# Own buffers and another pace for a depthwise convolution's products, and a layer norm that is queued when its last tile is whole

## The chip, the cores and the metric

The kernel runs on one core of a Trainium2 chip. Its time is the device time of one execution in microseconds; the forecast is made on the median of such runs. The core has TensorE (PE in the profile) for matrix products, VectorE (DVE), ScalarE (ACT) and GpSimd (POOL) for elementwise work, and SyncE (SP), whose queue issues nearly all loads here. Each engine runs its own instructions in order; semaphores tie them together. TensorE writes to PSUM, which this kernel cuts into eight buffers of 128 x 512 f32.

## The reference

One sequence of 512 tokens, 1024 channels, f32, goes through two blocks. The first block has a mixer (the part that the change touches), then 32 routed experts (the best two of one group for each token). The second block has an mLSTM mixer, a short convolution mixer and two squared-ReLU MLPs. The first mixer:

```python
h = rms_norm(x, norm_mix_g)
proj = h @ w_in + b_in                                   # 1024 -> 6144 columns
a, z, gate_logits = split(proj, [2048, 4096])
# conformer branch
a1, a2 = split(a, 2);  a = a1 * sigmoid(a2)
y = causal_depthwise_conv(a, conv_w, width=31) + conv_b  # 31 taps, each channel by itself
y_a = silu(layer_norm(y, ln_g, ln_b)) @ w_conv_out + b_conv_out
# spatial gating branch
u, v = split(gelu(z), 2);  v = layer_norm(v)
sv = einsum("hqk,bnkhc->bnqhc", w_s * mask, v) + b_s     # inside blocks of 128 tokens
y_b = (u * sv) @ w_sg_out + b_sg_out
g_a, g_b = split(sigmoid(gate_logits), 2)
x = x + (g_a * y_a + g_b * y_b) @ w_out + b_out
```

The layer norm of the conformer branch runs over all 1024 channels, so it needs every channel tile of the convolution.

## The kernel before, in words

Activations lie with 128 channels on the partitions and 512 tokens along the free axis, so a matrix of 1024 channels is eight tiles. A dense product makes one tile of 128 outputs by 512 tokens from eight tiles of input. Weights and inputs are held as pairs of f16 numbers, high and low, so each step is three products (`wh` with the high and with the low input, `wl` with the high one), and a tile is 24 products of 128 x 512. The weights arrive as f32 chunks by SP's queue; ScalarE makes the high part `wh` (L275) and VectorE the low part `wl` (L279), a chunk every two tiles.

The first mixer's dense products follow each other on TensorE in this order: `wa` (16 tiles, the convolution's input and its gate in turn), `wv` (8, tokens on partitions), `wu` (8), `wgb` and `wga` (8 each, the two gates), `wsgo`, `wco` and `wo` (8 each). ScalarE or VectorE empties each finished PSUM buffer: `ut` at L731 for `wu`, `gate` at L761 for both gates.

The order of all other work is made by a planner in the program itself. It keeps a clock `clk` that advances with the products as they are written down (512 columns count as 512/2400 us). `at(delay, fn)` hangs a piece of work into the order `delay` later on that clock. Two lists of fillers are worked off while dense products are written: one filler each time that the clock has passed a due time, which then moves on by `pace`. One list holds the even channel tiles of the convolution, the other the odd ones:

- even tiles: the sum stands in a PSUM buffer. One filler begins it on ScalarE, 30 fillers add one tap each on VectorE (L640, `yc<-ap,cw,yc`), and the last one copies it to SBUF on ScalarE (L647) and calls `conv_done`.
- odd tiles: one filler begins the sum on ScalarE (L627). Each of the 30 others is two instructions: ScalarE multiplies the shifted input by the tap's weight into a buffer `tap` (L622), and GpSimd adds that buffer to the sum (L623).

`conv_done` adds the finished tile to `ya` on GpSimd (L609, L611). The layer norm takes `ya` from there: `ln_mu` sums it over the partitions on TensorE (`cs`), `ln_sub` spreads the mean with four transposes (`bc`), subtracts it and adds up the squares, `ln_r` makes the reciprocal root, and `ln_out` multiplies, applies SiLU and makes the f16 pairs `ch` that the product `wco` reads.

`tap` buffers come from the pool `t2`, whose 48 buffers of 2 KB per partition serve nearly all working tiles of the mixer. Whoever takes a buffer of `t2` next waits until its last reader is done.

The spatial mixing is hung into `wgb`: for each of eight heads, four f32 products (`mix`) on TensorE, and on VectorE a scale and add out of PSUM (L744, `s`), a product with `ut` (L748), and the low part of an f16 pair (L750, `sh`), whose high part ScalarE makes (L749).

In the kernel before, fillers come every 1.5 (even) and 1.4 (odd) on the planner's clock. After `wgb` the program flushes the hung work, works off what is left of the fillers, and then hangs the layer norm at fixed places into `wga` (22, 25 and 40 after its begin) and `ln_out` 4 into `wsgo`.

Of the kernel before, what the change touches and what calls it, by code (L numbers as in the profile page):

```python
# [17 lines left out]
P = 128  # L18
T = 512
# [18 lines left out]
# ---------------------------------------------------------------- host layout  # L38
# [77 lines left out]
# ---------------------------------------------------------------- device  # L116
# [4 lines left out]
class Net:  # L121
    def __init__(self, ctx, tc, x, cols, rows, wd, we, wr, wsg, out):
        self.tc, self.nc = tc, tc.nc
        self.din = dict(x=x, cols=cols, rows=rows, wd=wd, we=we, wr=wr, wsg=wsg)
        self.out = out
        pool = lambda n, b, **k: ctx.enter_context(tc.tile_pool(name=n, bufs=b, **k))
        self.cp = pool("const", 1)
        self.t2p = pool("t2", 48)
        self.sp = pool("small", 2)
        self.wp = pool("w32", self.W32)  # L130
        self.hp = pool("whl", self.WHL)
        self.pp = pool("ps", 8, space=bass.MemoryType.PSUM)
        ctx.enter_context(tc.manual_schedule())
        self.uid = 0
        self.fillers = [], []
        self.due, self.pace = [0.0, 0.0], (1.0, 1.0)
        self.items = []
        for c in range(NDENSE):
            if c == N1:
                self.items += [("e", j) for j in range(NPAIR * 12)]  # L140
            self.items.append(("d", c))
        self.w32, self.whl, self.late = {}, {}, {}
        self.stop = len(self.items)
        self.nload = self.nsplit = self.cur = 0
        self.clk = 0.0
        self.last_split = -100.0
        self.queue = []
        self.open = False
        self.live = set()
# [7 lines left out]
    # ---- allocation  # L157
# [17 lines left out]
    # ---- the order of issue: TensorE's queue is the clock, the rest is hung into it  # L175
# [30 lines left out]
    # ---- weight stream  # L206
# [5 lines left out]
    def place(self, c):  # L212
        """where expert chunk c goes (the weight buffers, those of the split weights, or, at first, working tiles),
        and the chunk that was there before"""
        w, h, t = self.W32, self.WHL - 2, self.EXTRA
        rnd, rest = w + h + t + 2, w + h + 2
        if c < self.ROUNDS * rnd:
            r, before = c % rnd, c - rnd
        else:
            r = (c - self.ROUNDS * rnd) % rest  # L220
            before = c - rest
            if r >= w + h:
                r += t
            elif c < self.ROUNDS * rnd + rest:
                before -= t
        return "w" if r < w else "t" if w + h <= r < w + h + t else "h", before
# [16 lines left out]
    def more(self):  # L243
        """the working tiles are free to take expert chunks"""
        self.open = True
        self.loads()
# [67 lines left out]
    # ---- building blocks  # L314
# [5 lines left out]
    def dense(self, base, plan, rhs, evac, tail=None):  # L320
        """out tile m [P features, tokens] = W[:, m].T @ x over eight k tiles; two m tiles in a chunk.
        plan: (mode, tiles): "m" a tile at a time, "k" a group with k outside, "hk" as "k" for the first
        half of the tokens and as "m" for the second, "hh" the first half of all tiles, then the second"""
# [77 lines left out]
    def dense_tok(self, base, rhs, evac):  # L401
        """out [P tokens, 512 columns] for four token tiles, two column halves"""
# [19 lines left out]
    def colsum(self, tile_, s=FULL, dst=None):  # L422
        """[P tokens, tiles] in PSUM: the sum over partitions of a tile [P, tokens]"""
# [7 lines left out]
    def rsqrt(self, src, scale, eps, n, s="rs", pool=False):  # L431
        """1 / sqrt(src * scale + eps), a tile [P, n]"""
# [13 lines left out]
    def bcast(self, cols):  # L446
        """[P, n, P] in PSUM: each column as a row, on every partition"""
# [21 lines left out]
    # ---- constants  # L469
# [35 lines left out]
    # ---- first mixer  # L505
    def first_mixer(self):
# [6 lines left out]
        # the first chunks run on x * g, not yet divided by the norm  # L513
# [53 lines left out]
        # gated convolution branch: a pair of tiles, then the depthwise convolution as filler work,  # L567
        # the even tiles on VectorE with the sum in PSUM, the odd ones on ScalarE and GpSimd
# [3 lines left out]
        # layer norm over channels (partitions) of the convolution output  # L572
        ch = []

        def ln_mu():
            mu = self.sm([P, NT], s="mu")
            nc.vector.tensor_scalar(mu, self.colsum(ya), 1.0 / D, None, op0=OP.mult)
            st["mu"] = mu

        def ln_sub():  # L580
# [7 lines left out]
            st["a"] = a  # L588

        def ln_r():  # L590
            st["r"] = self.rsqrt(self.colsum(st["a"]), 1.0 / D, EPS, NT, pool=True)

# [13 lines left out]
        def conv_done(m):  # L606
# [3 lines left out]
            elif len(whole) > 2:  # L610
                nc.gpsimd.tensor_add(ya, ya, yc[m])  # L611

        def conv(m, ap):
            b = v("conv_b")[:, m:m + 1]
            yc[m] = self.t2([P, T], s="yc")
            if m % 2:
                y = yc[m]

                def tap(j):
                    q = self.t2([P, T], s="tap")  # L620
# [47 lines left out]
        # rows for the spatial gating  # L668
# [28 lines left out]
        self.pace = self.PACE[0]  # L697
        self.dense(CBASE["wa"], [("m", range(4, 16))], hn, ev_a)

        # spatial gating: v with tokens on partitions  # L700
# [10 lines left out]
        self.pace = self.PACE[1]  # L711
# [21 lines left out]
        self.pace = self.PACE[2]  # L733
        self.dense(CBASE["wu"], [("m", range(KD))], hn, ev_u)

        # spatial mixing inside blocks of 128 tokens, a head is a tile of channels
# [18 lines left out]
        # the two gates  # L755
# [8 lines left out]
        self.pace = self.PACE[3]  # L764
        self.dense(CBASE["wgb"], [("m", range(KD))], hn, ev_gate(5))
        self.flush()
        self.drain()
        self.at(22.0, ln_mu)
        self.at(25.0, ln_sub)
        self.at(40.0, ln_r)  # L770
        self.dense(CBASE["wga"], [("m", range(KD))], hn, ev_gate(4))
        self.flush()
# [4 lines left out]
        self.at(4.0, ln_out)  # L777
# [24 lines left out]
    PACE = ((1.5, 1.4), (1.5, 1.4), (1.5, 1.4), (1.5, 1.4))  # L802

    # ---- routed experts
# [16 lines left out]
    def pick(self, vals, n, top, s, out, tmp=None):  # L821
        """one-hot of the first of the n values that equals top, for each token tile"""
# [10 lines left out]
    def route_begin(self):  # L833
        """fp16 pairs of x * g with tokens on partitions, and the logits, tile by tile of x"""
# [55 lines left out]
    def moe(self):  # L890
# [10 lines left out]
        # products that nobody reads keep the clock of TensorE up until the routing is known  # L901
# [9 lines left out]
        # group, then the two best experts of the group  # L911
# [21 lines left out]
        # the rank of a choice among those of its expert, no slot's number where there is no choice  # L933
# [12 lines left out]
        def onehot(p):  # L946
            """tokens against the slots of a pair of experts, and room for the transposed matrix"""
# [7 lines left out]
        # weights of the choices and the reciprocal norm, fp16 pairs to be moved to slots  # L955
# [125 lines left out]
        def overflow():  # L1081
            """assignments beyond the slots of an expert, 64 more of each expert of a pair at a time"""
# [33 lines left out]
        def extra(p, d, ji, rc, o, f, pss):  # L1116
# [51 lines left out]
            # the weighted placing matrix, slots on partitions  # L1168
# [44 lines left out]
    # ---- second block  # L1213
# [12 lines left out]
    def pre_begin(self, g):  # L1226
        """fp16 pairs of x * g (not yet divided by the norm), and the squares of x"""
# [12 lines left out]
    def post_tail(self, rho=None, last=False):  # L1240
        """x += rms_norm(h) * g for a half of the tokens, where h = rho * d for each token"""
# [52 lines left out]
    def squares(self, r):  # L1294
        """the square of a column and its square, for post_tail"""
# [4 lines left out]
    def mlstm(self, last_scatter):  # L1300
# [87 lines left out]
        # gates: tokens on partitions, the sums over time of a chunk by a triangular product  # L1388
# [78 lines left out]
        # decay matrices and scores, keys on partitions  # L1467
# [291 lines left out]
```

## Time and profile before

| what | us |
|---|---|
| runs of the kernel | 1995.12, 1997.82, 1998.41 (median 1997.82) |
| span of the profiled execution | 1995.6 |
| TensorE busy in the span | 1928.2 (97%) |
| GpSimd busy in the span | 228.8 (11%), nearly all of it before 250 us |
| mean granted TensorE clock | 0.990 of full speed |

The profiled execution's own time is its span, 2.2 us under the median of the runs and inside their spread. In the profile's tables by windows, the columns are the stretch, its length, each engine's busy time with its instructions, the granted clock, the DMA engines' share and GB/s. A wait is listed as who waited for whom, in total, how often, and the longest. In a timeline, the first two columns are start and duration in us, and a bracket tells the idle time ahead and what ended it.

### The profile page before, as it was taken

Reading aid. Unit: us, or ns where it says so; the run is one execution under the profiler, and the core shown is the slowest. Engines: PE = TensorE matmul, PEld = TensorE weight load, DVE = VectorE, ACT = ScalarE, POOL = GpSimd, SP = SyncE. Lnnn points to the kernel's source line nnn. Section 1 sums busy time; section 2 is a strip of 40 time slices with the busy share of each in tenths; the row PEclk is TensorE's granted clock in tenths of the full one; section 3 lists DMA queues with packets and bytes.
Section 4 is the critical chain, followed back from the end, with each engine's and each line's share of the span. In section 5 each row is a group of like instructions: output and inputs, shape, how many; then the busy total and the mean of one; then the engine's idle time right before and its main releaser. Section 6 shows DMA issues by size and latency. Waiting matters only on the chain.

```text
span 1995.6 us, 26504 instructions
## 1 busy us (share of the span) xinstructions
PE 1928.2 (97%) x10925; PEld 988.1 (50%) x10926; DVE 990.0 (50%) x1515; ACT 716.6 (36%) x1026; POOL 228.8 (11%) x194
## 2 busy tenths in 40 slices
PE   8998799989999999998999999999999999999997
PEld 3444444454444444433555864444485467444445
DVE  7986775543233233236745674532267558444223
ACT  6867544231111111114444563322143236433120
POOL 1999900010000000001000000000000000000000
PEclk9999899999999999999999999999999999999999
DMA  6322133279999999996411233322313332332201
GB/s 249 129 104 85 42 127 125 84 277 352 388 396 400 372 413 413 413 413 234 148 64 64 86 106 106 106 106 85 126 44 127 106 106 85 106 106 103 109 22 43
DMA packets 82476, 347.59 MB, mean 174 GB/s; under 512 B 9776, under 2 KB 12080, under 8 KB 57776
## 3 DMA queue, kind: packets, MB, share of 16 engines
q1 hardware_dynamic: 79776, 343.12, 46.2%
q10 hardware_dynamic: 2576, 2.74, 0.5%
q8 instruction: 87, 1.43, 0.3%
q14 instruction: 37, 0.30, 0.0%
HBM read 343.73 MB, written 2.10 MB: 173 GB/s over the span
## 4 chain that ended last, share of the span: by engine, by line
PE 55%; DMA 6%; DVE 3%; ACT 1%; issue 0%; POOL 0%; DVEq 0%; SPq 0%; ACTq 0%
PE p L181 47%; DMA ewl<-in_we_dram 4%; DMA w<-in_we_dram 2%; PE y L181 2%; PE pg L181 1%; PE sc L181 1%; PE pu L181 1%; PE xs L181 1%; DVE wl L279 1%; PE num L181 1%; DVE x L1269 1%; DVE racc L464 0%; DVE d L1268 0%; PE bc L185 0%; DVE xh L1237 0%
## 5 line engine op out<-in xcount | busy, mean ns | idle before, releaser
L181 PEld LDWEIGHTS <-wh 128*128 128x128 f16 x4448 | 436.1, 98 | 407.5 <-issue 12.0
L181 PE MATMUL p<-xh,wh 128*128 128x512 f16 (+1 forms) x1824 | 468.6, 347 | 4.5 <-ACT xh L1233 2.2
L279 DVE SCALAR_TENSOR_TENSOR wl<-w,wh 128x2048 f16<-128x2048 f32 x130 | 304.3, 2353 | 121.4 <-ACT wh L275 119.3
L181 PEld LDWEIGHTS <-wl 128*128 128x128 f16 x2224 | 217.8, 98 | 204.5 <-issue 5.6
L181 PE MATMUL p<-xh,wl 128*128 128x512 f16 (+1 forms) x912 | 316.7, 347 | 1.7 <-DVE wl L279 1.7
L181 PE MATMUL p<-hid,wh 128*128 128x512 f16 (+1 forms) x1152 | 308.9, 356 | 0.0
L275 ACT ACTIVATE wh<-w 128x2048 f16<-128x2048 f32 x130 | 244.9, 1902 | 9.4 <-PE p L181 7.1
L181 PE MATMUL p<-hid,wl 128*128 128x512 f16 (+1 forms) x576 | 204.8, 356 | 0.0
L623 POOL TENSOR_TENSOR yc<-yc,tap 128x511 f32<-128x511 f32 (+14 forms) x120 | 181.3, 1511 | 51.2 <-ACT tap L622 42.3
L181 PE MATMUL p<-hn,wh 128*128 128x512 f16 x576 | 174.3, 384 | 3.1 <-ACT ut L731 2.1
L464 DVE TENSOR_TENSOR pacc<-pacc,sq 128x256 f32<-128x256 f32 (+1 forms) x41 | 21.4, 522 | 208.6 <-ACT sq L463 208.5
L181 PE MATMUL p<-hn,wl 128*128 128x512 f16 x288 | 110.2, 383 | 0.0
L1613 DVE TENSOR_TENSOR relu<-relu 128x512 f32<-128x512 f32 (+1 forms) x76 | 46.1, 606 | 126.2 <-ACT hid L1612 126.2
L463 ACT ACTIVATE sq<-p 128x256 f32<-128x256 f32 (+1 forms) x41 | 18.9, 461 | 229.5 <-PE p L181 229.3
L1611 ACT ACTIVATE relu<-p 128x512 f32<-128x512 f32 (+1 forms) x76 | 39.8, 524 | 159.4 <-PE p L181 159.4
L640 DVE SCALAR_TENSOR_TENSOR yc<-ap,cw,yc 128x511 f32<-128x511 f32 (+14 forms) x120 | 88.3, 736 | 8.1 <-ACT yc L636 5.4
L1043 DVE TENSOR_TENSOR h<-h,pu 128x512 f32<-128x512 f32 x16 | 11.0, 688 | 156.1 <-PE pu L181 110.3
L622 ACT ACTIVATE tap<-ap,cw 128x511 f32<-128x511 f32 (+14 forms) x120 | 78.1, 699 | 19.0 <-POOL yc L623 18.8
L1042 ACT ACTIVATE h<-pg,wd 128x512 f32<-128x512 f32 x16 | 11.0, 687 | 197.0 <-PE pg L181 116.2
L181 PE MATMUL p<-wh,xh 128*128 128x512 f16 x256 | 79.8, 379 | 0.0
L1077 DVE TENSOR_TENSOR x<-x,sc 128x512 f32<-128x512 f32 x128 | 78.4, 680 | 1.6 <-PE sc L181 1.2
L1066 ACT ACTIVATE yhl<-y,wd 128x512 f16<-128x512 f32 x32 | 22.0, 687 | 144.3 <-PE y L181 116.2
(378 smaller groups left out, 2526.9 us busy)
## 6 DMA issues: line engine op xcount, KB each, us to landing
w<-in_wd_dram SPq DMA_DIRECT2D x130, 1024.0 KB, 4.9
w<-in_we_dram SPq DMA_DIRECT2D x62, 1024.0 KB, 12.6
ewh<-in_we_dram SPq DMA_DIRECT2D x90, 512.0 KB, 11.4
ewl<-in_we_dram SPq DMA_DIRECT2D x90, 512.0 KB, 10.2
ex<-in_we_dram SPq DMA_DIRECT2D x160, 256.0 KB, 5.4
x<-in_x_dram SPq DMA_DIRECT2D x8, 256.0 KB, 6.5
w<-in_wd_dram SPq DMA_DIRECT2D x4, 512.0 KB, 6.7
out_dram<-x ACTq DMA_DIRECT2D x8, 128.0 KB, 1.7
```

The source lines that it names most:

```text
L181: self.nc.tensor.matmul(out, l, r, start=start, stop=stop)
L275: nc.scalar.activation(wh, t, AF.Copy, scale=WS)
L279: nc.vector.scalar_tensor_tensor(wl, t, WS, wh, op0=OP.mult, op1=OP.subtract)
L464: nc.vector.tensor_add(acc[:, s], acc[:, s], q)
L622: nc.scalar.activation(q[:, d:T], ap[:, 0:T - d], AF.Copy, scale=cw[:, j, m:m + 1])
L623: nc.gpsimd.tensor_add(y[:, d:T], y[:, d:T], q[:, d:T])
L640: V.scalar_tensor_tensor(y[0][:, d:T], ap[:, 0:T - d], cw[:, CONVW - 1 - d, m:m + 1], y[0][:, d:T], op0=OP.mult, op1=OP.add)
L1066: nc.scalar.activation(o[:, 0], y[q], AF.Copy, scale=wc)
L1077: V.tensor_add(xt[d], xt[d], ps)
L1269: (nc.gpsimd if i and last and k in (0, 2, 4) else nc.vector).tensor_add(x, x, d)
L1611: nc.scalar.activation(a, ps, AF.Relu, scale=IWS)
L1613: nc.vector.tensor_mul(a, a, a)
```

## The change

1. A pool of its own, `tap`, with six buffers of 2 KB, serves the `tap` tiles. `t2` keeps its 48 buffers for the rest. The room comes from a smaller scratch area for dynamically described DMA (`dynamic_dma_scratch_size=1024`).
2. Fillers come every 1.7 (even) and 1.75 (odd) on the planner's clock, and the lists run on through `wgb` and `wga`. What is left is worked off after `wga`; the flush and the working off between the two gates are gone.
3. The layer norm is no longer hung at fixed places. `conv_done` hangs `ln_mu` 5 after the eighth tile, `ln_mu` hangs `ln_sub` 3 later, that hangs `ln_r` 14 later, and that `ln_out` 4 later.

```diff
         self.sp = pool("small", 2)
+        self.tapp = pool("tap", 6)
...
             st["mu"] = mu
+            self.at(3.0, ln_sub)
...
             st["a"] = a
+            self.at(14.0, ln_r)
 
         def ln_r():
             st["r"] = self.rsqrt(self.colsum(st["a"]), 1.0 / D, EPS, NT, pool=True)
+            self.at(4.0, ln_out)
...
             elif len(whole) > 2:
                 nc.gpsimd.tensor_add(ya, ya, yc[m])
+            if len(whole) == KD:
+                self.at(5.0, ln_mu)
...
                 def tap(j):
-                    q = self.t2([P, T], s="tap")
+                    q = self.tapp.tile([P, T], F32, name=self.name("tap"), tag="tap")
...
-        self.pace = self.PACE[0]
+        self.pace = self.PACE
         self.dense(CBASE["wa"], [("m", range(4, 16))], hn, ev_a)
...
-        self.pace = self.PACE[3]
         self.dense(CBASE["wgb"], [("m", range(KD))], hn, ev_gate(5))
-        self.flush()
+        self.dense(CBASE["wga"], [("m", range(KD))], hn, ev_gate(4))
         self.drain()
-        self.at(22.0, ln_mu)
-        self.at(25.0, ln_sub)
-        self.at(40.0, ln_r)
-        self.dense(CBASE["wga"], [("m", range(KD))], hn, ev_gate(4))
-        self.flush()
...
-        self.at(4.0, ln_out)
         self.dense(CBASE["wsgo"], [("m", range(KD))], sh, ev_sg)
...
-    PACE = ((1.5, 1.4), (1.5, 1.4), (1.5, 1.4), (1.5, 1.4))
+    PACE = 1.7, 1.75
...
-    nc = bacc.Bacc("TRN2", target_bir_lowering=False, num_devices=1)
+    nc = bacc.Bacc("TRN2", target_bir_lowering=False, num_devices=1, dynamic_dma_scratch_size=1024)
```

The changed file also drops comments, so its lines are numbered differently: the tap on ScalarE is L628 there (L622 before), the add on GpSimd L629 (L623), the emptying of `wu` L736 (L731) and of the gates L765 (L761), the high part of `sh` L753 (L749), its low part L754 (L750), the scale and add of the spatial mixing L748 (L744), and the product with `ut` L752 (L748).

ScalarE where `wu` ends and the first gate begins, before; a bracket names the engines' semaphores on which the instruction waits:

```order
L731 ACTIVATE ut_1723<-p_1681,cols_83 128x512 [waits PE_49,Pool_49]
L622 ACTIVATE tap_1738<-ap_970,cw_206 128x500 [waits Pool_49]
L275 ACTIVATE wh_1741<-w_279_1352 128x2048 [waits DMAHW0_49]
L622 ACTIVATE tap_1765<-ap_970,cw_206 128x499 [waits Pool_49]
L622 ACTIVATE tap_1772<-ap_970,cw_206 128x498 [waits Pool_49]
L622 ACTIVATE tap_1782<-ap_970,cw_206 128x497
L749 ACTIVATE sh_1725<-s_1760 128x512 [waits DVE_49,Pool_49]
L761 ACT_TABLE_LOAD [waits PE_49]
L761 ACTIVATE gate_1789<-p_1733,cols_83 128x512 [waits Pool_49]
```

The same place on ScalarE now:

```order
L736 ACTIVATE ut_1651<-p_1614,cols_86 128x512 [waits PE_49]
L628 ACTIVATE tap_1665<-ap_770,cw_209 128x490 [waits Pool_49]
L276 ACTIVATE wh_1668<-w_264_1301 128x2048 [waits DMAHW0_49]
L628 ACTIVATE tap_1693<-ap_770,cw_209 128x489 [waits Pool_49]
L628 ACTIVATE tap_1702<-ap_770,cw_209 128x488 [waits Pool_49]
L753 ACTIVATE sh_1653<-s_1688 128x512 [waits DVE_49]
L628 ACTIVATE tap_1713<-ap_770,cw_209 128x487 [waits Pool_49]
L765 ACT_TABLE_LOAD
L765 ACTIVATE gate_1716<-p_1661,cols_86 128x512 [waits PE_49]
```

The emptying of PSUM (`ut`, `gate`) no longer waits for GpSimd itself; the taps ahead of it still do. The taps here belong to the third odd tile now (`ap_770`), to the last one before (`ap_970`).

ScalarE from the last taps to the layer norm's first square (`lsq`), now:

```order
L628 ACTIVATE tap_2224<-ap_937,cw_209 128x485 [waits Pool_49]
L628 ACTIVATE tap_2237<-ap_937,cw_209 128x484 [waits Pool_49]
L628 ACTIVATE tap_2250<-ap_937,cw_209 128x483 [waits Pool_49]
L765 ACTIVATE gate_2257<-p_2220,cols_86 128x512 [waits PE_49]
L628 ACTIVATE tap_2263<-ap_937,cw_209 128x482 [waits Pool_49]
L276 ACTIVATE wh_2267<-w_400_1897 128x2048 [waits DMAHW6_49]
L653 ACTIVATE yc_856<-yc_1826 128x512 [waits DVE_49]
L765 ACTIVATE gate_2296<-p_2259,cols_86 128x512 [waits PE_49]
L461 ACTIVATE lsq_2332<-yc_405 128x512 [waits DVE_49]
```

Before, the last taps stood in the first gate, and between the copy of the last even tile and that square stood eight instructions:

```order
L647 ACTIVATE yc_880<-yc_1705 128x512 [waits DVE_49,Activation_49]
L761 ACTIVATE gate_2140<-p_2113,cols_83 128x512 [waits PE_49,Pool_49]
L275 ACTIVATE wh_2146<-w_371_1744 128x2048 [waits DMAHW4_49]
L761 ACTIVATE gate_2173<-p_2142,cols_83 128x512 [waits PE_49]
L761 ACTIVATE gate_2200<-p_2175,cols_83 128x512 [waits PE_49]
L275 ACTIVATE wh_2206<-w_400_1867 128x2048 [waits DMAHW5_49]
L761 ACTIVATE gate_2233<-p_2202,cols_83 128x512 [waits PE_49]
L761 ACTIVATE gate_2260<-p_2235,cols_83 128x512 [waits PE_49,Activation_49]
L275 ACTIVATE wh_2266<-w_424_1979 128x2048 [waits DMAHW6_49]
L460 ACTIVATE lsq_2302<-yc_402 128x512 [waits DVE_49]
```

One gate's emptying now stands between that copy and the square; the taps have moved from the first gate product into the second. SP's queue is the same in both kernels throughout, and from the product `wco` on so is the order on every engine.

More of the change, by code (lines that the diff above doesn't have):

```diff
@@ L709, in ev_v @@
             vt[t, h] = z
-        self.pace = self.PACE[1]
         self.dense_tok(CBASE["wv"], hn, ev_v)
@@ L731, in ev_u @@
             nc.scalar.activation(ut[m], ps, AF.Gelu, scale=IWS, bias=v("b_in", 2)[:, m:m + 1])
-        self.pace = self.PACE[2]
         self.dense(CBASE["wu"], [("m", range(KD))], hn, ev_u)
```

## The prediction

> **What bounds the kernel now.** I read the page's busy times first, then the first 440 us by windows, then who waited for whom there, then the timelines of the engines named.
>
> ```profile
> PE 1928.2 (97%) x10925; PEld 988.1 (50%) x10926; DVE 990.0 (50%) x1515; ACT 716.6 (36%) x1026; POOL 228.8 (11%) x194
> ```
>
> TensorE is busy nearly throughout, so a change in the mixer pays only where TensorE stands still or runs slow there. By windows of 20 us, three of them:
>
> ```profile
> 160.00:180.00 20.00, 20.00 (x94) 9.02 (x93) 12.96 (x15) 15.48 (x20) 19.06 (x14) 1.00 0.32 104
> 220.00:240.00 20.00, 13.41 (x53) 7.15 (x52) 16.95 (x16) 11.89 (x18) 19.06 (x13) 0.83 0.16 53
> 260.00:280.00 20.00, 20.00 (x100) 9.74 (x99) 13.49 (x12) 10.20 (x11) 1.27 (x1) 1.00 0.47 159
> ```
>
> The first number after the length is TensorE's busy time: full before 180 and after 260, 13.4 of 20 at 220, where GpSimd is at its limit (19.06, fifth) and the granted clock is 0.83. TensorE's waits in the mixer name the cause:
>
> ```profile
> PE mix L181 <- ACT gate L761: 7.9, 2, 4.6
> PE mix L181 <- DVE s L744: 3.2, 1, 3.2
> PE mix L181 <- ACT ut L731: 3.0, 1, 3.0
> PE p L181 <- ACT ut L731: 2.1, 1, 2.1
> PE mix L181 <- ACT yc L647: 1.0, 1, 1.0
> PE p L181 <- DVE s L744: 0.5, 1, 0.5
> ```
>
> TensorE waits for PSUM buffers that ScalarE or VectorE has not emptied: 17.7 us in all. And these two wait for GpSimd:
>
> ```profile
> ACT tap L622 <- POOL yc L623: 18.8, 22, 2.2
> ACT ut L731 <- POOL yc L623: 4.5, 6, 1.6
> ```
>
> A tap on ScalarE takes a `t2` buffer that GpSimd has yet to read; what stands behind it in ScalarE's order, the emptying of PSUM, is held too. GpSimd itself never pauses:
>
> ```profile
> 48.96 52.78 POOL L623 TENSOR_TENSOR yc<-yc,tap 128x511 f32<-128x511 f32 x31 [42.30 <-ACT tap L622]
> 247.44 1.26 POOL L611 TENSOR_TENSOR ya<-ya,yc 128x512 f32<-128x512 f32 x1
> ```
>
> From 48.96 to 248.70 it does the 120 adds of the odd tiles and six sums into `ya` of 1.27 each: (199.74 - 7.6) / 120 = 1.60 us an add, and 52.78 / 31 = 1.70 in the first stretch. The planner offers one every 1.4 on its clock. GpSimd is the bound of this stage, and the queue in front of it has grown until ScalarE stands.
>
> The pauses also cost clock; in windows of 5 us those under 1.00 are:
>
> ```profile
> 195.00:200.00 5.00, 2.16 (x9) 1.55 (x9) 0.12 (x1) 3.76 (x6) 4.77 (x5) 0.87 0.49 187
> 200.00:205.00 5.00, 5.00 (x22) 2.37 (x22) 1.51 (x2) 2.17 (x4) 4.76 (x4) 0.79 0.00 0
> 215.00:220.00 5.00, 3.97 (x15) 2.65 (x16) 2.02 (x3) 2.10 (x3) 4.69 (x5) 0.66 0.19 80
> 225.00:230.00 5.00, 4.08 (x15) 2.70 (x16) 3.48 (x4) 4.75 (x6) 4.69 (x5) 0.66 0.00 0
> 235.00:240.00 5.00, 4.14 (x15) 2.50 (x16) 4.93 (x6) 2.49 (x5) 4.76 (x4) 0.66 0.63 213
> ```
>
> The missing clock is 0.13 + 0.21 + 3 x 0.34 = 1.36, times 5 us = 6.8 us, 1.7 for each of four pauses. **The stage loses 17.7 + 6.8 = 24.5 us**, and that is the most the change can give.
>
> **The change part by part.** *The pace.* A product takes a third of the distance of two triples:
>
> ```profile
> 182.62 0.59 PE L181 MATMUL p<-hn,wh 128*128 128x512 f16 x2
> 183.27 0.59 PE L181 MATMUL p<-hn,wh 128*128 128x512 f16 x2
> 189.66 1.16 PE L181 MATMUL mix<-wsg,vt 128*128 128x128 f32 x8 [2.99 <-ACT ut L731]
> 190.66 0.60 PE L181 MATMUL p<-hn,wh 128*128 128x512 f16 x2
> ```
>
> 0.65 / 3 = 0.216 us; a head's `mix` takes 1.00. From the first to the last add of the odd tiles the order of the changed kernel has 940 products and eight heads: 940 x 0.216 + 8 = 211 us for 119 distances, 1.77 each. GpSimd needs 1.60, and with seven sums 1.67, so 94% of what it is offered; the queue no longer grows. ScalarE's taps should find their buffers free, with room for six adds (10 us). The even taps come slower as well, which only relieves VectorE before `wgb`.
>
> *Six own buffers.* The waits of `ut` and `gate` for GpSimd leave the order. The pool has less depth than the taps used of `t2` before, which costs nothing while GpSimd keeps up; the third rival is that it doesn't. The smaller scratch area is costed at nothing: the page's list of DMA issues names the queues of SP and ScalarE alone.
>
> *The spread over both gates.* The adds now run beside the whole spatial mixing and beyond. VectorE's groups while GpSimd was busy (182 to 248 us), then after (248 to 268):
>
> ```profile
> L279 DVE SCALAR_TENSOR_TENSOR wl<-w,wh 128x2048 f16<-128x2048 f32 x3 | 8.8, 2940 | 6.2 <-ACT wh L275 6.2
> L750 DVE TENSOR_TENSOR sh<-s,sh 128x512 f16<-128x512 f32 x4 | 6.8, 1712 | 0.0
> L748 DVE TENSOR_TENSOR s<-s,ut 128x512 f32<-128x512 f32 x6 | 6.8, 1132 | 0.2
> L744 DVE SCALAR_TENSOR_TENSOR s<-mix,cols,bsg 128x512 f32<-128x512 f32 x6 | 4.5, 746 | 11.0 <-POOL yc L623 11.0
> ```
> ```profile
> L279 DVE SCALAR_TENSOR_TENSOR wl<-w,wh 128x2048 f16<-128x2048 f32 x2 | 4.6, 2281 | 0.0
> L748 DVE TENSOR_TENSOR s<-s,ut 128x512 f32<-128x512 f32 x3 | 2.7, 915 | 0.1
> L750 DVE TENSOR_TENSOR sh<-s,sh 128x512 f16<-128x512 f32 x4 | 2.7, 682 | 0.0
> L640 DVE SCALAR_TENSOR_TENSOR yc<-ap,cw,yc 128x491 f32<-128x491 f32 x1 | 0.7, 733 | 0.0
> ```
>
> From the first head's scale to the last even tap the order now gives VectorE eight heads, six `wl` and 37 taps. Beside GpSimd: 8 x (0.746 + 1.132 + 1.712) + 6 x 2.94 + 37 x 0.733 = 28.7 + 17.6 + 27.1 = 73.4 us; alone: 18.7 + 13.7 + 27.1 = 59.5. TensorE passes 265 products and seven heads there, 57.2 + 7 = 64.2 us. So VectorE ends between on time and 9.2 us late. (L744 and the taps are the same in both.) In `wgb` that lateness is harmless: of eight PSUM buffers a tile takes two there, one for its products and one for a head, so a buffer is taken again two or three tiles (24 x 0.216 = 5.2 us each) after its last use, and ScalarE can be held as long.
>
> *The layer norm's begin* is where it tells. Before, 104 products (22 us) lay between the last `ya` add and `cs`; now 13. Three terms:
>
> ```profile
> 265.89 0.72 DVE L640 SCALAR_TENSOR_TENSOR yc<-ap,cw,yc 128x482 f32<-128x482 f32 x1
> 266.70 0.60 ACT L647 ACTIVATE yc<-yc 128x512 f32<-128x512 f32 x1 [4.25 <-DVE yc L640]
> 267.44 1.27 POOL L611 TENSOR_TENSOR ya<-ya,yc 128x512 f32<-128x512 f32 x1 [18.73 <-ACT yc L647]
> 294.40 0.95 PE L181 MATMUL cs<-ones,lsq 128*128 128x1 f32 x8
> 297.09 0.16 DVE L443 SCALAR_TENSOR_TENSOR rs<-rsw,rsy 128x4 f32<-128x4 f32 x1
> ```
>
> By VectorE: the last tap to the end of `ya` is 268.71 - 266.61 = 2.1 us, the last tap to `cs` is 40 products, 8.6 us; 9.2 us late gives a wait of 2.7, on time gives none. By GpSimd: until ScalarE's last `sh` copy, which waits for VectorE, the sum beside GpSimd is 8 x 1.878 + 7 x 1.712 + 3 x 2.94 + 19 x 0.733 = 49.8 us against 146 products and seven heads, 38.5, so ScalarE is up to 11.3 us late there; 17 taps are still to come, 17 x 1.60 + 2 x 1.27 = 29.7 us, and `cs` stands 159 products, 34.3 us, behind that copy: 29.7 + 11.3 - 34.3 = 6.7 us of waiting, or none. I take the middle, 3.3: the adds overlap the mixing, but a held ScalarE starves GpSimd and so frees VectorE. A pause of 2.99 kept the clock (at 189.66), one of 3.24 lost it, so half of 1.7 goes on top. The reciprocal root takes 297.25 - 294.40 = 2.85 us and one `wl` (2.28) may stand ahead of it; 21 products, 4.5 us, lie before its transposes: 0 to 0.6, taken as 0.3. The rest of the layer norm has its old distances (66 products from the mean's transposes to the second `cs`) and 156 products before `wco`.
>
> **The sum.** -24.5 + 3.3 + 0.9 + 0.3 = -20.0 us. What follows keeps its order and its loads are tied to the mixer's own progress, so all of it moves up. The profiled execution's 1995.6 becomes 1975.6; it lies 2.2 under the median of the runs, so I forecast **1977.8** on the median of 1997.8. With the waits' two ends the same kernel gives 1973.3 (none) to 1982.3 (6.7 + 1.7 + 0.6).
>
> **The rivals.**
>
> *No new wait:* VectorE is on time because the adds are starved or lie elsewhere; all 24.5 are won, 1973.3. For it: TensorE stood at 20.00 of 20 from 260 to 280, though the last even tap came only at 265.89. Against it: 13 products are 2.8 us, about the 2.1 us that the copy and the add alone take.
>
> *VectorE shut out in full.* The row has `sh` at 1.71 beside GpSimd and 0.68 alone, 1.03 more, less than one GpSimd sum (1.27). If each of the 22 instructions with two SBUF inputs (eight products, eight `sh`, six `wl`) waited for a whole one: 59.5 + 22 x 1.27 = 87.4 us, 23.2 late, `cs` waits 16.7 and loses 1.7: 6.1 are won, 1991.7. The Trainium skill's page "SBUF — State Buffer" (Who interferes with whom) says so: a VectorE instruction with two SBUF inputs and a GpSimd one that reads SBUF exclude each other, and the one that comes second blocks fully. The rows agree in direction, but not that each pays a whole instruction: `s<-s,ut` pays 0.2.
>
> *GpSimd still too slow, with less room (the other side).* If an add took 1.70 or more throughout, as in its first 31 (from there, with the sums, the 1.77 are used up), the queue grows again, and six buffers hold ScalarE sooner than `t2` did, in `wv` and `wu` already. To lose more than the 24.5, an add must take 1.91; at 2.0 the last one is 36 us late, and 36 - 24.5 gives 2009. Against it: no long stretch has shown more than that 1.70, and the mean of all 120 is 1.60. For it: adds and VectorE's work now collide for longer.
>
> *The waits only move.* With an add at 1.90 the same 24 us come back before `cs`: 1997, no change.
>
> **How the numbers follow.** Forecast with one short wait at `cs` 0.45; no wait 0.29; VectorE shut out, or a wait between that and the forecast, 0.17; only moved 0.04; slower 0.05. A change under 0.2% (4 us) is about what cannot be told from none. The first three are faster: 0.91; same 0.04; slower 0.05. The range begins at 1973.3 less the runs' own spread below the median (2.7), 1971; it reaches past 1982.3 halfway to 1991.7, to 1987, since the second rival may come in part.
>
> **What would show it.** Right: no wait of ScalarE's `tap` for GpSimd over a microsecond or so, TensorE at 20.00 of 20 with clock 1.00 from 180 to 240, and one wait of `cs` for `ya` of 0 to 7 us near 270. Wrong: TensorE waiting for `gate` or `s` in `wgb` (VectorE's lateness is not absorbed), `tap` waiting in `wa` (GpSimd over 1.70), `sh` beyond 1.7, or a stage after `wco` that takes longer than before, which no term here allows for.

## The result, and the profile after

| | before | after |
|---|---|---|
| median of the runs, us | 1998.12 (4 runs) | 1988.78 (4 runs) |
| profiled execution (span), us | 1995.6 | 1984.4 |
| time after / before | | 0.995, 95% interval 0.9938 to 0.9962 |

The changed kernel is faster by 9.3 us. The forecast was 1977.8, a gain of 20.0; somewhat under half of that came, and the time lies 1.8 us above the range.

TensorE's waits between 40 and 330 us are one row now; the six of before are gone, and with them everything that waited for `gate`, `ut` and `s`:

```profile
PE cs L182 <- POOL ya L615: 13.5, 1, 13.5
```

By windows of 20 us (stretch, length, busy time with instructions of PE, PEld, DVE, ACT and POOL, granted clock, DMA share, GB/s):

```profile
160.00:180.00 20.00, 20.00 (x95) 9.07 (x93) 15.30 (x16) 20.00 (x28) 17.49 (x13) 1.00 0.40 147
220.00:240.00 20.00, 20.00 (x95) 9.05 (x93) 19.75 (x21) 13.38 (x20) 16.86 (x10) 1.00 0.21 61
240.00:260.00 20.00, 15.44 (x72) 6.79 (x70) 16.98 (x19) 15.46 (x21) 19.06 (x13) 1.00 0.41 150
260.00:280.00 20.00, 11.04 (x45) 5.86 (x46) 4.95 (x8) 2.14 (x5) 8.52 (x6) 0.66 0.16 52
```

At 220, where TensorE was busy for 13.41 of 20 at a clock of 0.83, it is now full at 1.00. The loss stands at 255 to 269 instead. TensorE's timeline there, with the last product ahead of the pause, and a window over the 6 us behind it:

```profile
255.06 0.38 PE L182 MATMUL p<-hn,wl 128*128 128x512 f16 x1
268.96 1.87 PE L182 MATMUL cs<-ones,ya 128*128 128x1 f32 x8 [13.53 <-POOL ya L615]
270.69 1.01 PE L182 MATMUL p<-hn,wh 128*128 128x512 f16 x2
...
274.44 0.60 PE L182 MATMUL p<-hn,wh 128*128 128x512 f16 x2
```
```profile
268.90:274.90 6.00, 5.94 (x20) 3.26 (x21) 0.16 (x1) 0.00 (x0) 0.01 (x1) 0.54 0.00 0
```

The pause is 13.53 us, and (1 - 0.54) x 6.00 = 2.8 us of clock go after it. So of the 24.5 us of waits and clock that the change took away, 16.3 came back at this one place, which leaves 8.2; the medians show 9.3. The traces of the mixer alone agree: from the 101st dense product (at 33 us) to the 1641st (at 394 us) TensorE takes 370.4 us before and 360.9 after. GpSimd is what `cs` waits for. Its timeline from the first add to the last sum into `ya`, middle left out, and its group of adds:

```profile
49.34 51.53 POOL L629 TENSOR_TENSOR yc<-yc,tap 128x511 f32<-128x511 f32 x30 [42.55 <-ACT tap L628]
...
141.56 3.82 POOL L629 TENSOR_TENSOR yc<-yc,tap 128x488 f32<-128x488 f32 x3 [1.02 <-ACT tap L628]
...
235.83 30.40 POOL L629 TENSOR_TENSOR yc<-yc,tap 128x498 f32<-128x498 f32 x17 [0.25 <-ACT tap L628]
266.31 2.60 POOL L615 TENSOR_TENSOR ya<-ya,yc 128x512 f32<-128x512 f32 x2
```
```profile
L629 POOL TENSOR_TENSOR yc<-yc,tap 128x511 f32<-128x511 f32 (+14 forms) x120 | 193.1, 1609 | 57.2 <-ACT tap L628 48.7
```

The same group in the trace of before:

```profile
L623 POOL TENSOR_TENSOR yc<-yc,tap 128x511 f32<-128x511 f32 (+14 forms) x120 | 181.3, 1511 | 51.2 <-ACT tap L622 42.3
```

The same 120 adds are 11.8 us longer in all. A stretch of three takes 1.27 each (at 141.56), the last 17 take 1.79 each.

### The profile page after: what moved, and what is told of

Its sections match the earlier page's. It is cut to its first block, busy times and chain, and to the rows that moved or that the text cites. A ratio compares the mean times of both kernels' runs of the same rounds, so it can differ in the third digit from the quotient of the medians.

```text
span 1984.4 us, 26464 instructions
## 1 busy us (share of the span) xinstructions
PE 1923.0 (97%) x10925; PEld 984.9 (50%) x10926; DVE 989.8 (50%) x1515; ACT 715.0 (36%) x1026; POOL 239.4 (12%) x194
## 4 chain that ended last, share of the span: by engine, by line
PE 58%; DMA 4%; DVE 3%; ACT 1%; issue 0%; POOL 0%; DVEq 0%; ACTq 0%; SPq 0%
PE p L182 48%; DMA ewl<-in_we_dram 3%; PE y L182 2%; PE pg L182 2%; PE pu L182 1%; PE sc L182 1%; PE xs L182 1%; DMA w<-in_we_dram 1%; DVE wl L280 1%; PE num L182 1%; DVE x L1266 1%; DVE d L1265 0%; PE bc L186 0%; DVE racc L465 0%; DVE xh L1234 0%
## 5 line engine op out<-in xcount | busy, mean ns | idle before, releaser
L629 POOL TENSOR_TENSOR yc<-yc,tap 128x511 f32<-128x511 f32 (+14 forms) x120 | 193.1, 1609 | 57.2 <-ACT tap L628 48.7
L628 ACT ACTIVATE tap<-ap,cw 128x511 f32<-128x511 f32 (+14 forms) x120 | 79.6, 701 | 22.0 <-POOL yc L629 21.9
L1063 ACT ACTIVATE yhl<-y,wd 128x512 f16<-128x512 f32 x32 | 21.9, 687 | 144.4 <-PE y L182 116.5
## 6 DMA issues: line engine op xcount, KB each, us to landing
ewh<-in_we_dram SPq DMA_DIRECT2D x90, 512.0 KB, 11.4
```

The source lines that it names most:

```text
L628: nc.scalar.activation(q[:, d:T], ap[:, 0:T - d], AF.Copy, scale=cw[:, j, m:m + 1])
L629: nc.gpsimd.tensor_add(y[:, d:T], y[:, d:T], q[:, d:T])
L1063: nc.scalar.activation(o[:, 0], y[q], AF.Copy, scale=wc)
```

## What makes an add long

Two rows of the changed kernel lie side by side at 155 us, the low part of a weight chunk on VectorE and one add on GpSimd:

```profile
155.38 2.28 DVE L280 SCALAR_TENSOR_TENSOR wl<-w,wh 128x2048 f16<-128x2048 f32 x1
155.58 3.21 POOL L629 TENSOR_TENSOR yc<-yc,tap 128x511 f32<-128x511 f32 x1 [0.34 <-ACT tap L628]
157.58 3.90 DVE L646 SCALAR_TENSOR_TENSOR yc<-ap,cw,yc 128x511 f32<-128x511 f32 x5
158.96 3.96 POOL L629 TENSOR_TENSOR yc<-yc,tap 128x510 f32<-128x510 f32 x3 [0.17 <-ACT tap L628]
```

The add that begins inside `wl` ends 1.13 us after it, that is, it does its work when `wl` is done: 3.21 us instead of some 1.28. The three adds beside five even taps, whose sum stands in PSUM, take 1.27 each (3.96 us hold three of them and two gaps of 0.07). Counted over each trace (an add counts as long above 1.8 us):

```
                                wl between first     long adds        other adds
kernel                          and last add         number, mean us  mean us
before                          16                   15, 3.19         1.272
the change                      21                   21, 3.15         1.282
layer norm later                22                   22, 3.16         1.283
wl with one SBUF input          21                   20, 2.08         1.274
wl in four pieces               81 pieces            none             1.406
```

Nearly each `wl` lengthens one add, by 1.9 us, and the others keep their 1.28 (in the trace of before, the sixteenth `wl` held a sum into `ya` instead, which took 3.3 us). So the price of an add is not a constant: it is 1.28 plus 1.9 for every `wl` that TensorE's progress calls for meanwhile. One `wl` belongs to 48 products, 48 x 0.216 = 10.4 us of an unhindered TensorE. The change lets TensorE run, and for that very reason more `wl` fall on the same 120 adds: 21 - 15 = 6 more long ones, 6 x 1.9 = 11.4 of the 11.8 us. The Trainium skill's page "SBUF — State Buffer" (Who interferes with whom) says that a VectorE instruction with two SBUF inputs and a GpSimd one that reads SBUF shut each other out, and that the one that comes second blocks fully; for the adds the trace agrees, one full wait for each `wl`.

## The experiments

Theory 1: `cs` stands too early in TensorE's order for GpSimd, which runs behind its places by a lag from the start, `wl` and held taps; the pace does the rest of the good, the buffers none. Rival: VectorE is late with the last even tile (the forecast's first path), or the own buffers are what freed ScalarE.

**The layer norm alone, 16 later.**

```diff
-                self.at(5.0, ln_mu)
+                self.at(21.0, ln_mu)
```

> The changed kernel with one number changed: the layer norm's first sum is hung 21 instead of 5 behind the eighth tile, so that 16 us more of dense products stand ahead of it. Theory 1 (GpSimd is 13.5 us late at that place and nothing else is wrong): the wait of cs for ya vanishes or falls under 1 us, and the 13.5 us with some 2.7 us of half clock come back: 1971 to 1975 us. Theory 2 (what is late there makes something else late next, the pairs ch for wco or the gates' buffers): a wait of several us appears before wco, and the time stays above 1980.

Measured: 1972.02 us, ratio to before 0.9874 (0.9858 to 0.9891). TensorE waits for nothing from 40 to 330 us. Its windows, and GpSimd's last rows:

```profile
240.00:260.00 20.00, 20.00 (x95) 9.04 (x94) 16.98 (x20) 15.47 (x21) 19.00 (x13) 1.00 0.45 154
260.00:280.00 20.00, 20.00 (x100) 9.88 (x99) 9.69 (x9) 8.28 (x10) 11.55 (x6) 1.00 0.47 158
```
```profile
236.66 32.58 POOL L629 TENSOR_TENSOR yc<-yc,tap 128x498 f32<-128x498 f32 x17 [0.24 <-ACT tap L628]
269.32 2.62 POOL L615 TENSOR_TENSOR ya<-ya,yc 128x512 f32<-128x512 f32 x2
```

GpSimd is no sooner done than in the change (271.94 against 268.91), but nobody waits for it. The gain on before is 25.0 us, the 24.5 that the forecast gave as the most. This kernel beats both.

**The change with its taps in `t2` again, alone and with the later layer norm.**

```diff
-                    q = self.tapp.tile([P, T], F32, name=self.name("tap"), tag="tap")
+                    q = self.t2([P, T], s="tap")
```

> The changed kernel with the tap tiles back in the shared pool of 48; the pace and the layer norm's places as changed. Theory 1 (GpSimd's capacity sets the end, the buffers do not): the wait of cs stays at 12 to 15 us, no waits for gate or ut come back, 1986 to 1992 us. Theory 2 (the six own buffers removed the waits of ut and gate for GpSimd): those waits come back, 5 us or more of them in the first gate, and the time is 1993 or above.

> The change with the layer norm hung 21 instead of 5 after the eighth tile (as in the run with the later layer norm alone, 1972.0 us), and with the taps' buffers taken from t2 again. Theory: the six own buffers contribute nothing, the even pace and the place of the layer norm are all of it: 1970 to 1974 us, no wait of cs for ya, no wait of TensorE for gate or ut. Rival: the own buffers keep ut and gate from waiting for GpSimd once the layer norm's wait no longer slows things: without them 2 to 8 us of such waits come back and the time is 1975 to 1981 us.

Measured: 1987.5 us alone (0.9943, 0.9921 to 0.9965) and 1972.23 with the later layer norm (0.9868, 0.9852 to 0.9884), the same as with the own buffers in both cases. TensorE's waits in the first of the two are one row:

```profile
PE cs L182 <- POOL ya L615: 9.6, 1, 9.6
```

In the second there is none. The expectation for the first missed in size, 9.6 us of waiting and not 12 to 15. The trace shows where the difference begins: with the 48 buffers of `t2`, ScalarE's taps hardly wait for GpSimd,

```profile
ACT tap L628 <- POOL yc L629: 3.8, 3, 2.1
```

where it is 21.9 us with six, and from the 101st dense product to the 1641st TensorE takes 357.5 us instead of 360.9. The median hides these 3.4 us: the experts' stage behind the mixer, which no edit touches, takes 492.4 to 495.8 us in the ten traces of this case, and 2.4 longer in this one than in the change's; the stages behind it take another 1.8 longer. So the six own buffers win nothing. With the early layer norm they cost some 3 us of the mixer in these two traces; with the later one both kernels take 344.5.

**The kernel before with the six buffers alone** (old distances, old places of the layer norm; the smaller scratch area, which makes the room, comes with them).

```diff
+        self.tapp = pool("tap", 6)
...
-                    q = self.t2([P, T], s="tap")
+                    q = self.tapp.tile([P, T], F32, name=self.name("tap"), tag="tap")
...
-    nc = bacc.Bacc("TRN2", target_bir_lowering=False, num_devices=1)
+    nc = bacc.Bacc("TRN2", target_bir_lowering=False, num_devices=1, dynamic_dma_scratch_size=1024)
```

> The kernel before with the taps in six buffers of their own and nothing else: the old pace, the old places of the layer norm. Theory 1 (GpSimd's capacity is what matters): it is offered more than it can do, ScalarE is held at the taps as before, sooner since there are fewer buffers, and TensorE pauses in wu and the first gate for 17 us or more: 1996 to 2006 us. Theory 2 (the shared buffers were the fault): the waits for ut and gate shrink to a few us, under 1988.

Measured: 1996.3 us, ratio 0.9992 (0.9983 to 1.0002): no difference. The rows of waits:

```profile
ACT tap L623 <- POOL yc L624: 40.2, 43, 3.8
...
PE mix L182 <- ACT gate L762: 7.6, 2, 4.4
PE p L182 <- ACT ut L732: 3.0, 2, 2.3
```

`ut` and `gate` no longer wait for GpSimd themselves, but the taps ahead of them in ScalarE's queue do, longer than before (40.2 us against 18.8), so TensorE stands as it did.

**The change with the old distances** (1.5 and 1.4, the layer norm hung so that `cs` stands, but for three products, where it does in the run with the later layer norm).

```diff
-                self.at(5.0, ln_mu)
+                self.at(45.0, ln_mu)
...
-    PACE = 1.7, 1.75
+    PACE = 1.5, 1.4
```

> The change with the old distances of the fillers (1.5 and 1.4 instead of 1.7 and 1.75), and the layer norm hung 45 after the eighth tile, so that cs stands at the same place of TensorE's order as in the run with the later layer norm. Theory: the pace is what removes the stalls; at 1.4 offered against some 1.5 to 1.6 needed GpSimd falls behind by 0.1 to 0.2 us an add, six buffers are full after 50 adds or so, and ScalarE is held as before: taps wait 20 to 45 us in all, TensorE waits 10 to 20 us for gate, ut or s, and the time is 1986 to 1998 us. Rival: what helps is that the flush and the working off between the two gates are gone and that nothing else is left waiting for t2: then 1971 to 1976 us, as with the new pace.

Measured: 1995.29 us, ratio 0.9982 (0.9972 to 0.9992). Theory 1 holds: the taps wait 40.2 us for GpSimd again, and TensorE waits as before:

```profile
PE mix L182 <- ACT gate L765: 6.9, 2, 4.4
PE mix L182 <- ACT ut L736: 3.3, 1, 3.3
PE p L182 <- DVE wl L280: 2.9, 1, 2.9
```

From the run with the later layer norm this differs in the pace alone (`cs` stands three products, 0.6 us, earlier), and the ratios stand 1.1% apart (0.9982 and 0.9874): the pace is worth some 21 us once `cs` stands late enough.

**`wl` with one SBUF input.** In the first mixer VectorE makes `wl` from the f32 weight alone; the subtraction of the high part is left out, so the low parts are not those of the reference's weights.

```diff
-                nc.vector.scalar_tensor_tensor(wl, t, WS, wh, op0=OP.mult, op1=OP.subtract)
+                if i < N1:
+                    nc.vector.tensor_scalar(wl, t, WS / 4096.0, None, op0=OP.mult)
+                else:
+                    nc.vector.scalar_tensor_tensor(wl, t, WS, wh, op0=OP.mult, op1=OP.subtract)
```

> The changed kernel with the first mixer's low weight parts made by a VectorE instruction that reads one operand from SBUF and not two (the weights scaled; the subtraction of the high part is left out, so the low parts are not the real ones). Theory 1 (GpSimd's late end comes from adds that a wl blocks for its whole length, 20 adds at 3.2 us against 1.24 for the rest): the blocked adds take 1.24 plus at most the new instruction's length; if that is 1.1 us long or does not block, GpSimd saves 20 us or more, ends before 255, cs waits less than 1 us, and the time is 1970 to 1976 us. Theory 2 (GpSimd ends late because ScalarE, held behind VectorE's mixing, hands it the taps late): adds stay late all the same, cs waits 8 us or more, 1982 to 1988.

Measured: 1971.85 us, ratio 0.9877 (0.9858 to 0.9897), no wait of `cs`. The groups of `wl` and of the adds, and the last sums:

```profile
L281 DVE TENSOR_SCALAR wl<-w 128x2048 f16<-128x2048 f32 x26 | 39.8, 1533 | 0.0
```
```profile
L632 POOL TENSOR_TENSOR yc<-yc,tap 128x511 f32<-128x511 f32 (+14 forms) x120 | 169.0, 1408 | 66.9 <-ACT tap L631 59.3
```
```profile
252.95 2.62 POOL L618 TENSOR_TENSOR ya<-ya,yc 128x512 f32<-128x512 f32 x2
```

A shorter `wl` makes the long adds shorter with it (2.08 us), the adds take 24 us less, GpSimd ends 13.3 us sooner, and the pause is gone without moving `cs`. One SBUF input does not free GpSimd entirely: 20 adds are still held. But the edit also shortens VectorE's own work, by 1.0 us for each `wl` (1.53 against 2.56 in the mean), and ScalarE's last `sh` copy, which waits for VectorE, comes 4.0 us behind its place instead of 13.7. So this run does not separate the two theories of its expectation: both engines got faster at once.

**`wl` in four pieces of 512 columns.**

```diff
-                nc.vector.scalar_tensor_tensor(wl, t, WS, wh, op0=OP.mult, op1=OP.subtract)
+                for q in range(4 if i < N1 else 1):
+                    c = slice(512 * q, 512 * (q + 1)) if i < N1 else slice(0, 2048)
+                    nc.vector.scalar_tensor_tensor(wl[:, c], t[:, c], WS, wh[:, c], op0=OP.mult, op1=OP.subtract)
```

> The change with each low part wl of the first mixer's weights made in four instructions of 512 columns instead of one of 2048. Theory: an add that meets a wl is held for the rest of that VectorE instruction; pieces of 0.6 to 0.7 us hold it for one piece at most, then GpSimd goes ahead and the next piece waits for it. So no add takes over 2.0 us (3.2 before), the 120 adds take 165 to 180 us instead of 193, cs waits 0 to 4 us instead of 13.5, VectorE's pieces take longer (2.6 to 4.5 us for four), and the time is 1970 to 1977 us. Rival: VectorE's queue issues the pieces so close behind each other that GpSimd does not get between them: adds of 3 us remain, cs waits 12 to 15 us, the time is 1985 to 1990 us.

Measured: 2012.86 us, ratio 1.0072 (1.0055 to 1.0088), slower than before. The adds did what the theory said (168.8 us in all, none above 1.8), the time did the opposite:

```profile
152.06 4.48 POOL L631 TENSOR_TENSOR yc<-yc,tap 128x491 f32<-128x491 f32 x3 [3.96 <-ACT tap L630]
152.59 5.10 DVE L282 SCALAR_TENSOR_TENSOR wl<-w,wh 128x512 f16<-128x512 f32 x4
```
```profile
L282 DVE SCALAR_TENSOR_TENSOR wl<-w,wh 128x512 f16<-128x512 f32 x88 | 107.2, 1277 | 2.7 <-ACT wh L276 2.7
L631 POOL TENSOR_TENSOR yc<-yc,tap 128x511 f32<-128x511 f32 (+14 forms) x120 | 168.8, 1406 | 100.9 <-ACT tap L630 93.4
```

Add and piece now alternate, and VectorE pays: four pieces take 5.10 us here and 4.9 in the mean (88 pieces, 107.2 us, are 22 `wl`), where one uncut `wl` took 2.3 to 3.3, 2.56 in the mean. The change's row:

```profile
L280 DVE SCALAR_TENSOR_TENSOR wl<-w,wh 128x2048 f16<-128x2048 f32 x24 | 61.5, 2560 | 10.8 <-ACT wh L276 10.8
```

The expectation's 2.6 to 4.5 us for four was too low, and that this would make VectorE late was not in it. VectorE late holds ScalarE, ScalarE holds the taps, and GpSimd, the engine that was to be helped, is left without work:

```profile
ACT yc L655 <- DVE yc L648: 29.6, 3, 18.2
ACT vt L715 <- DVE vt L714: 29.2, 8, 6.6
ACT sh L755 <- DVE s L754: 21.6, 6, 6.9
```

The wait of `cs` is still there (14.8 us), and TensorE also waits 9.5 us for `gate` and 5.6 for `vt`.

**The small loads later.** Eight loads that ScalarE's queue issues from 36 to 41 us move behind the first four tiles.

```diff
-        self.at(16.0, load_rows)
...
-        self.at(20.0, sums)
+        self.at(30.0, load_rows)
+        self.at(60.0, sums)
```

> The change with the eight small loads that ScalarE's queue issues at 36 to 41 us moved behind the first four tiles (30 on the planner's clock, in the order's middle of wa), and the sums that read them 60 behind instead of 20. Theory: these issues hold ScalarE for 4.2 us and put off the first tap; without them the first add starts at 44 to 47 us instead of 49.3, GpSimd ends as much sooner, cs waits 9 to 12 us instead of 13.5, and the time is 1984 to 1988 us. Rival: the first tap waits for the product before it and for VectorE, not for ScalarE: it starts at 49 as before, cs waits 13 to 14 us, the time is 1988 to 1990 us.

Measured: 1985.6 us, ratio 0.9931 (0.9914 to 0.9948); the interval overlaps that of the change. The first add and the wait:

```profile
47.91 13.62 POOL L629 TENSOR_TENSOR yc<-yc,tap 128x511 f32<-128x511 f32 x7 [40.83 <-ACT tap L628]
```
```profile
PE cs L182 <- POOL ya L615: 10.8, 1, 10.8
```

The start moves by 1.4 us only (by 2.4 against TensorE, which runs 1.0 later in this trace), less than expected: two splits of weights, a table load and the gate's sigmoid still stand ahead of the first tap. The wait of `cs` shrinks by 2.7, as theory 1 expects: what is late at the start is still late at the end. By the time alone this run does not decide.

## Why the prediction was right or wrong

**Right.** GpSimd as the bound of the stage, ScalarE held by it, and TensorE held by ScalarE: the even pace takes all of these waits away, and TensorE runs at 20.00 of 20 with clock 1.00 from 180 to 240, as the prediction said the right case would look. The ceiling was right too: 24.5 us forecast as the most, 25.0 measured with the later layer norm (25.9 from the 101st to the 1641st dense product of the traces). The part on the own buffers gave them the waits of `ut` and `gate`; those went, but the runs show that the pace took them, since without it the taps ahead hold ScalarE just as long.

**A sign of "wrong" that did appear.** No tap should have waited more than a microsecond or so. Taps waited 21.9 us, 16.4 of it before 112 us, most of that beside `wa`, which ends at 97 us:

```profile
ACT tap L628 <- POOL yc L629: 21.9, 16, 2.8
```
```profile
ACT tap L628 <- POOL yc L629: 16.4, 11, 2.8
```

(The second row is the same view from 45 to 112 us.) The prediction named this as the sign of a GpSimd over 1.70, and it was at 1.72 in its first 30 adds. So the queue did grow at first and was full at six. TensorE did not feel it there, but ScalarE did, and VectorE through it: between 45 and 272 us VectorE waited 25.4 us for ScalarE's `wh`, `sg` and `vt`, against 15.2 with the taps in `t2`. The forecast had set the smaller depth of the pool at nothing, "while GpSimd keeps up"; it did not keep up.

**Wrong: the term "3.3" for the wait of `cs`.** It measured 13.5, and its clock 2.8 instead of 0.9. The forecast had two paths to `cs`. VectorE's came out near its late end: its last five even taps ran from 252.72 to 256.48, and with the 2.1 us behind them `cs` would have waited 3.1 by that path, where 2.7 was the most allowed. That is some ten us ahead of the last sums into `ya` at 266.31. The path by GpSimd decided, and its bound, 29.7 + 11.3 - 34.3 = 6.7, was itself exceeded. By its own terms:

- 29.7 for the last 17 adds and two sums: from 235.83 to 268.91 it was 33.1, +3.4. Four of the 17 met a `wl`, so they took 1.79 each and not 1.60.
- 11.3 for the lateness where these 17 begin: 34.3 us ahead of the pause's begin (255.4) is 221.1; they began at 235.83, 14.7 late, +3.4.
- together 14.7 + 33.1 - 34.3 = 13.5, the measured wait. And of a bound of 6.7 the forecast then took the middle.

Where these last 17 adds begin, GpSimd had no work left. It waited for a tap, and ScalarE ahead of that for VectorE's `s`:

```profile
229.38 0.63 ACT L753 ACTIVATE sh<-s 128x512 f16<-128x512 f32 x1 [6.22 <-DVE s L752]
```
```profile
230.75 3.12 POOL L629 TENSOR_TENSOR yc<-yc,tap 128x501 f32<-128x501 f32 x2 [1.96 <-ACT tap L628]
234.33 1.25 POOL L629 TENSOR_TENSOR yc<-yc,tap 128x499 f32<-128x499 f32 x1 [0.46 <-ACT tap L628]
```

So the 14.7 is ScalarE's lateness behind VectorE's mixing, as in the forecast's 11.3. That bound let the mixing begin on time; VectorE in fact began the first head's `s` 4.2 us late, and its lateness grew by 9.2 over the mixing, to 13.4 at the last. The other runs follow the same sum. In this table the first two columns say how many us behind TensorE's passing of its place in the order an instruction begins, the third how long after the moment 34.3 us ahead of the place of `cs`; third plus fourth less 34.3 is the wait:

```
                          first s    last sh    17 adds   adds and   wait
kernel                    begins     begins     begin     two sums   of cs
the change                4.2        13.7       14.7      33.1       13.5
the loads later           1.5        11.0       12.0      33.1       10.8
taps in t2                0.3         8.6       10.9      32.9        9.6
wl with one SBUF input    0.2         4.0        4.7      28.8       none
```

**The step behind it: "GpSimd needs 1.60 ... so 94% of what it is offered".** Two things were missing. First, the 1.60 was a mean over a stage in which TensorE stood still for a good part, with 16 `wl` beside 120 adds; the change removes the standing still and so adds `wl`. With 1.28 for an add, 0.07 for the gap behind it, 1.9 for a `wl` and one `wl` in 10.4 us, 211 us of offers hold 20 `wl`: 120 x 1.35 + 20 x 1.9 = 200 us, 1.67 an add, 1.74 with the seven sums. That is 98% of 1.77, and nothing is left to make up for a late start. Second, there was a late start. The sum went from the first add to the last and never asked how far behind its place the first one ran. Set against the moment at which TensorE passes an add's place in the order, the end of the add comes later by (us):

```
add number                      1      29     57     85     99     120
the change                      12.2   19.1    9.9   14.3   15.3   16.1
the loads later                  9.8   17.7    6.3   11.6   12.6   13.4
wl with one SBUF input          12.4   12.9    2.2    3.2    4.5    1.7
```

The lag is there at the first add, since ScalarE has splits, a table load and eight issues ahead of the first tap (it ran at 48.5, its place passed at 38.4), and the change never works it off. It does not stay with GpSimd alone: the full pool hands it to ScalarE and VectorE. GpSimd waited some 8 us for ScalarE behind its first add (48.7 - 42.5 for taps, 2.0 for a copy), and there its lag was ScalarE's own: 5.5 us of it up to 165 us, where ScalarE waited for VectorE's `vt` (17.1 us in all) and then worked without a pause (20.00 of 20 at 160), and 2.7 us in the mixing, where it waited for `s`. With one SBUF input, adds of 1.41 and a shorter `wl` on VectorE together work the lag off, and that run has no pause.

**The rivals.** The one of VectorE shut out in full gave 1991.7 with a wait of 16.7, close to what came. But that is close in number only. VectorE paid too, though less than a whole sum each time: the two of its rows that have both inputs in SBUF took 1.39 and 1.25 us in the mixing, against 0.68 and 0.92 alone, and its path alone would have given a wait of 3.1.

```profile
L754 DVE TENSOR_TENSOR sh<-s,sh 128x512 f16<-128x512 f32 x8 | 11.1, 1387 | 0.0
L752 DVE TENSOR_TENSOR s<-s,ut 128x512 f32<-128x512 f32 x8 | 10.0, 1246 | 0.3
```

GpSimd paid at 1.9 for each `wl`. The trace of before had it: 15 adds of 3.2 us among 105 of 1.27. The prediction priced the exclusion in one direction only, from VectorE's rows, and took GpSimd's side as a mean. "No new wait" missed here, but is the run with the later layer norm.

**Left open:** how the 10.0 us by which the run with one SBUF input begins its last 17 adds sooner divide between GpSimd's shorter adds and VectorE's shorter `wl`, and whether a first tap that is earlier by more than 1.4 us would be carried to the end in full.

## What to carry to other kernels

Where two engines shut each other out, price both sides, and price them per meeting: count how many of the one's instructions fall on the other's work at the rate after the change, since a mean duration from a stalled stage holds only while the stage is stalled. Where work is placed by an order written ahead, read how far behind its place the first piece runs before setting a consumer close behind the last. A shallow pool between two engines passes lateness back to the one that fills it, and from there to whoever waits for that one. A consumer whose result is needed much later (here the layer norm, 156 products ahead of `wco`) costs nothing to place late, and a good deal to place early.

## What the runs showed of the hardware

- An add on GpSimd (128 x 482 to 511 f32, both inputs in SBUF) takes 1.20 to 1.28 us alone or beside VectorE instructions that read PSUM and one SBUF tile, and 3.2 when it begins inside a `wl` with two SBUF inputs. The `wl` takes 2.28 us when it comes first and up to 3.34 when an add is already running.
- Beside a `wl` with a single SBUF input (`tensor_scalar`, f32 to f16, 1.53 us) it takes 2.08: held as well. The Trainium skill's page "SBUF — State Buffer" (Who interferes with whom) lets `tensor_scalar` contend when it runs in a two-port mode; no run here shows in which mode it ran.
- Cut in four, the exclusion becomes an exchange: add, piece, add, piece, 1.28 us for a piece (waiting for adds included) and 1.41 for an add in the mean (4.48 us for the three adds at 152.06, 5.10 for the four pieces at 152.59), so a whole `wl` takes VectorE 4.9 us instead of 2.56.
- After the pause of 13.53 us TensorE had half its clock for 5.5 us of products (268.96 to 274.44), a loss of 2.8 us. Before, pauses of 3.24, 3.35 and 4.58 us had cost 1.7 each, and two close together, of 2.15 and 0.98, as much; one of 2.99 alone cost none.
